# Recurrent layer of a two-layer encoder: two weight remainders ordered behind the first two convolutions, and the first block's gates 2 to 4 steps later

## The chip, the cores and the metric

One Trainium2 chip, one core. The metric is the device time of one execution in microseconds (us); lower is better. All arithmetic is in 32-bit floating point: a weight or an activation is split into a rounded part `hi` and a remainder `lo`, and each product is made of three matmuls (hi·hi, hi·lo, lo·hi).

## The reference, cut to what matters

256 tokens of width 2048 pass through two layers. Layer 0 mixes tokens by attention, layer 1 by a recurrent block; each is followed by a gated feed-forward part. The change lies at the start of the recurrent block:

```python
def recurrent_mixer(h, w_in, conv_w, conv_b, w_a, b_a, w_i, b_i, lam, w_out):
    xy = h @ w_in
    xb, yb = jnp.split(xy, 2, axis=-1)
    yb = jax.nn.gelu(yb, approximate=True)
    xb = depthwise_conv_centred(xb, conv_w, conv_b)
    h_fwd = rg_lru(xb, w_a[0], b_a[0], w_i[0], b_i[0], lam[0], reverse=False)
    h_bwd = rg_lru(xb, w_a[1], b_a[1], w_i[1], b_i[1], lam[1], reverse=True)
    out = (h_fwd + h_bwd).astype(h.dtype) * yb
    return out @ w_out
```

`rg_lru` puts xb through two block-diagonal 256x256 products (the gates), sigmoids them, and scans over the tokens.

## The kernel before, in words

The channels of the recurrent layer go in 8 blocks of 256 (`Block`, L945), two tiles of 128 channels each. While TensorE projects the two x tiles and the two y tiles of one round, the gates, decays and scans of the block before are strewn in between. What the steps of the prediction touch:

- **Weights.** `half()` (L218) takes the next half tile of weights (128x1024) from a fixed list. `load_half` (L126) loads it by SyncE's queue into `raw`, ScalarE casts it to `hi` (L141), VectorE makes the remainder `lo` (L143). Each of raw, hi and lo has 5 buffers, so a load waits for the remainder of five halves earlier. A half holds 8 tiles of 128x128; a tile costs three matmuls (L410, L411, L412: hi·hi, hi·lo of the activation, lo·hi), together one **step** of a counter (`step`, L251).
- **First round.** Before any block there is a round that makes only two x tiles (`project_two`, L426), whose sums lie in two PSUM banks. Then a tiny TensorE product (L542) spreads the row norms, and ScalarE copies it to `nrb` (L544).
- **Convolution.** `conv_branch` (L905): VectorE scales the sum by the norm (`cb`, L910), ScalarE makes the first tap (L912), VectorE the other three (L915: two into the accumulator, one into `xc`), then the cast `xs` (L439) and its remainder (L440). The two convolutions of the first round need the norm and so start only after it; their `xs` feed the gates of block 0.
- **Gates.** `Block.gates` (L956): 12 matmuls (L410 to L412 with `xs` and the gate weights `ghi`, `glo`) into a bank `pm`, of which there are 4. Gates, decays, scans and the finish of a block are functions put on a waiting list, each to be issued by TensorE's program a stated number of steps after the block began: `WHEN_FIRST` for block 0, which begins right behind the product that spreads the norm.
- **Order.** TensorE runs in the order in which the code is written. The order on the other engines is chosen at build time by a scheduler, which may be bound by hand: `not_after(i, ahead)` (L118) notes that the remainder (or, with "act", the cast) of the half taken `ahead` halves later must stand behind instruction i on its engine; `settled` (L121) applies it in `load_half`.

## Time and profile before

| what | us |
|---|---|
| median of 3 runs | 1962.69 |
| lowest and highest of them | 1962.0 and 1963.04 |
| span of the profiled execution | 1962.8 |
| TensorE busy in it | 1955.2 |
| VectorE busy | 1737.4 |
| ScalarE busy | 1357.9 |

The profiled execution's own time is its span, the time from its first to its last instruction. TensorE's matmuls are pipelined: one of 128x256 is listed with 0.28 us but the next one starts 0.12 us after it. So a busy TensorE isn't yet one at full speed, and the starts of successive matmuls tell more than their durations. The granted clock is listed beside the busy times of each stretch (1.00 is full speed).

### The profile page before, as it was taken

The page shows a single profiled execution, that of the slowest core. Times are in us where ns is not written, and L with a number is a line of the kernel's source. Part 1 is how long each engine was busy: PE and PEld are TensorE (multiplying, and loading weights), DVE is VectorE, ACT ScalarE, POOL GpSimd, SP SyncE. Part 2 cuts the span into 40 slices and gives each one's busy share as a digit, 9 for nine tenths or more (in the row PEclk, how much of TensorE's full clock was granted, in tenths as well). Part 3 has the DMA queues.
Part 4 walks back from the last instruction along what each step waited for, and adds up shares of the span by engine and source line. Part 5 has one row for each costly group of instructions (what it writes and reads, how often), then busy time and mean ns, then how long its engine had stood idle before and what let it go on. Part 6 is the DMA issues. An engine that isn't in the chain of part 4 may idle for free.

```text
span 1962.8 us, 27715 instructions
## 1 busy us (share of the span) xinstructions
PE 1955.2 (100%) x9641; PEld 1659.9 (85%) x9641; DVE 1737.4 (89%) x2374; ACT 1357.9 (69%) x2075; POOL 233.7 (12%) x333
## 2 busy tenths in 40 slices
PE   9999999999999999999999999999999999999999
PEld 8888888888888888888899998888888888888887
DVE  6777889999999989999778986999998999989997
ACT  6666767665677556777689986767756776567763
POOL 0011000010011100101034331001101010011010
PEclk9999999999999999999999999999999999999999
DMA  8544667687677876776545556567767777777784
GB/s 333 186 147 138 202 204 240 219 258 246 209 246 242 269 245 214 228 234 232 197 166 184 190 166 209 193 203 243 245 233 239 240 240 255 229 245 236 234 261 163
DMA packets 136364, 434.95 MB, mean 222 GB/s; under 512 B 15264, under 2 KB 16160, under 8 KB 135968
## 3 DMA queue, kind: packets, MB, share of 16 engines
q1 hardware_dynamic: 109296, 360.01, 53.3%
q0 software_dynamic: 26784, 73.15, 14.7%
q8 instruction: 76, 1.25, 0.3%
q14 instruction: 64, 0.52, 0.1%
q10 hardware_dynamic: 144, 0.02, 0.0%
HBM read 431.02 MB, written 2.10 MB: 221 GB/s over the span
## 4 chain that ended last, share of the span: by engine, by line
PE 96%; ACT 2%; DVE 1%; issue 1%; DMA 0%; DVEq 0%; ACTq 0%
PE acc L357 60%; PE pm L357 12%; PE acc L273 10%; PE acc L410 3%; PE acc L411 3%; PE acc L412 3%; PE pm L273 1%; PE pm L411 1%; PE pm L412 1%; PE pm L410 1%; ACT tf L871 1%; DVE lo L143 1%; PE pm L748 1%; PE pm L780 1%; PE pm L766 0%
## 5 line engine op out<-in xcount | busy, mean ns | idle before, releaser
L143 DVE TENSOR_TENSOR lo<-raw,hi 128x1024 fp32r<-128x1024 f32 (+1 forms) x613 | 736.7, 1227 | 87.8 <-ACT hi L141 81.9
L141 ACT CAST hi<-raw 128x1024 fp32r<-128x1024 f32 (+1 forms) x613 | 627.4, 1046 | 255.3 <-PE acc L357 93.0
L357 PE MATMUL acc<-hi,xg 128*128 128x512 f32 x1920 | 612.9, 389 | 0.0
L357 PEld LDWEIGHTS acc<-hi,xg 128*128 128x128 f32 x1920 | 360.4, 188 | 74.7
L357 PE MATMUL acc<-hi,act 128*128 128x512 f32 x1258 | 402.1, 390 | 0.8 <-DVE act L879 0.5
L357 PE MATMUL acc<-lo,xg 128*128 128x512 f32 x960 | 373.5, 389 | 0.0
L357 PEld LDWEIGHTS acc<-hi,act 128*128 128x128 f32 x1258 | 236.0, 188 | 50.6 <-DVE act L879 1.4
L357 PE MATMUL acc<-lo,act 128*128 128x512 f32 x629 | 244.8, 389 | 0.0
L357 PEld LDWEIGHTS acc<-lo,xg 128*128 128x128 f32 x960 | 180.2, 188 | 37.5
L327 ACT CAST wxh<-raw 128x1024 fp32r<-128x1024 f32 x93 | 97.8, 1052 | 110.8 <-DVE raw L325 110.8
L871 ACT COPY tf<-tb 32x256 f32<-32x256 f32 x352 | 142.0, 404 | 5.5 <-DVE tb L865 1.6
L410 PE MATMUL acc<-xg,hi 128*128 128x256 f32 x512 | 145.6, 284 | 0.0
L411 PE MATMUL acc<-xg,hi 128*128 128x256 f32 x512 | 145.4, 284 | 0.0
L412 PE MATMUL acc<-xg,lo 128*128 128x256 f32 x512 | 145.2, 284 | 0.0
L357 PEld LDWEIGHTS acc<-lo,act 128*128 128x128 f32 x629 | 118.2, 188 | 23.8
L323 ACT CAST wxh<-wx 128x512 fp32r<-128x512 f32 x93 | 57.7, 621 | 110.4 <-DVE wx L320 78.2
L322 ACT CAST hi<-sr 128x1024 fp32r<-128x1024 f32 x93 | 97.7, 1051 | 39.2 <-PE acc L357 28.4
L329 DVE TENSOR_TENSOR wxl<-raw,wxh 128x1024 fp32r<-128x1024 f32 x93 | 112.7, 1211 | 6.9 <-ACT wxh L327 6.9
L326 DVE TENSOR_TENSOR lo<-sr,hi 128x1024 fp32r<-128x1024 f32 x93 | 113.1, 1216 | 0.0
L305 POOL DMA_DIRECT2D sr<-in_w_up_dram x64 | 35.6, 557 | 651.0 <-DVE lo L326 482.6
L273 PE MATMUL acc<-hi,xg 128*128 128x512 f32 x320 | 109.0, 401 | 0.3 <-ACT hi L141 0.3
L410 PEld LDWEIGHTS acc<-xg,hi 128*128 128x128 f32 x512 | 98.7, 193 | 0.0
(212 smaller groups left out, 3330.4 us busy)
## 6 DMA issues: line engine op xcount, KB each, us to landing
raw<-in_w_gate_dram SPq DMA_DIRECT2D x176, 512.0 KB, 5.4
raw<-in_w_down_dram SPq DMA_DIRECT2D x147, 512.0 KB, 5.5
raw<-in_w_up_dram SPq DMA_DIRECT2D x112, 512.0 KB, 5.6
sr<-in_w_up_dram POOLq DMA_DIRECT2D x64, 512.0 KB, 4.9
raw<-in_w_in_dram SPq DMA_DIRECT2D x64, 512.0 KB, 4.3
raw<-in_w_qkv_dram SPq DMA_DIRECT2D x46, 512.0 KB, 4.4
raw<-in_w_o_dram SPq DMA_DIRECT2D x32, 512.0 KB, 3.5
wx<-in_w_up_dram SPq DMA_DIRECT2D x64, 256.0 KB, 4.7
```

The lines of the kernel that those rows point to most:

```text
L141: newest["cast"] = in_line("act", act.copy(hi[:, sl, :], raw[:, sl, :]))
L143: rest = in_line("dve", dve.tensor_tensor(lo[:, sl, :], raw[:, sl, :], hi[:, sl, :].bitcast(F32), ALU.subtract))
L273: pe.matmul(accs[a], x, wt[:, k, :], start=(k0 + k == 0 and n == 0), stop=(end and k == 1 and n == 2))
L322: in_line("act", act.copy(hi, raw))
L326: settled(in_line("dve", dve.tensor_tensor(lo, raw, hi[:].bitcast(F32), ALU.subtract)), taken[0] - 1)
L327: in_line("act", act.copy(xh[:, 1:, :], r1))
L329: in_line("dve", dve.tensor_tensor(xl[:, 1:, :], r1, xh[:, 1:, :].bitcast(F32), ALU.subtract))
L357: pe.matmul(acc, a, b, start=id(acc) not in begun, stop=last and i == 2)
L410: pe.matmul(o, hi, x[:, :S], start=start, stop=False)
L411: pe.matmul(o, hi, x[:, S:], start=False, stop=False)
L412: pe.matmul(o, lo, x[:, :S], start=False, stop=stop)
L871: n = act.copy(f[32 * i : 32 * i + 32, q::4, :, :], b[32 * q : 32 * q + 32, :, i, :, :])
```

## The change

Two edits. In `conv_branch`, for the first two channel tiles (ct 0 and 1), the first tap on ScalarE and the remainder of `xs` on VectorE are now noted by `not_after(..., 3)`: the cast and the remainder of the fourth weight half after that point stand behind them on ScalarE and VectorE. In `WHEN_FIRST`, the first three gates of block 0 are issued after 28, 34 and 38 steps and no longer after 24, 30 and 36; the fourth stays at 42, and so does all that follows it.

```diff
-WHEN_FIRST = (24, 30, 36, 42) + WHEN[4:]
+WHEN_FIRST = (28, 34, 38, 42) + WHEN[4:]
...
     def split(dst, src):
         i = dve.tensor_copy(dst[:, :S], src)
-        dve.tensor_tensor(dst[:, S:], src, dst[:, :S].bitcast(F32), ALU.subtract)
+        newest["split"] = dve.tensor_tensor(dst[:, S:], src, dst[:, :S].bitcast(F32), ALU.subtract)
         return i
...
         xc = tmp("xc", bufs=4)
-        act.activation(run, b[:, 0:S], AF.Identity, bias=col("conv_b", ct), scale=col("conv_w", ct))
+        i = act.activation(run, b[:, 0:S], AF.Identity, bias=col("conv_b", ct), scale=col("conv_w", ct))
+        if ct < 2:
+            not_after(i, 3, "act")
         for k in range(1, 4):
             o = xc if k == 3 else run
             dve.scalar_tensor_tensor(o, b[:, k : k + S], col("conv_w", KT * k + ct), run, ALU.mult, ALU.add)
         xs = tmp("xs", (P, 2 * S), F32R, bufs=4)
-        split(xs, xc)
+        i = split(xs, xc)
+        if ct < 2:
+            not_after(newest["split"], 3)
         return xc, xs
```

The numbers of the tiles in the rows below are running numbers of the program; a few change with the order. The four weight halves that matter here are hi_9019/lo_9020 (now hi_8994/lo_8995), hi_9087/lo_9088 (now hi_9062/lo_9063), hi_9142/lo_9143 and hi_9207/lo_9208.

VectorE, from the remainder of the third half after the first round; xs_8850 and xs_8862 are the two operands of the gates, cb_8841 and cb_8853 the inputs of their convolutions. Before:

```order
L143 TENSOR_TENSOR lo_9020<-raw_9018,hi_9019 128x1024
L910 TENSOR_TENSOR cb_8841<-acc_8714,nrb_8836 128x256
L910 TENSOR_TENSOR cb_8853<-acc_8715,nrb_8836 128x256
L143 TENSOR_TENSOR lo_9088<-raw_9086,hi_9087 128x1024
L915 SCALAR_TENSOR_TENSOR acc_8714<-cb_8841,pk,acc_8714 128x256
L143 TENSOR_TENSOR lo_9143<-raw_9141,hi_9142 128x1024
L915 SCALAR_TENSOR_TENSOR acc_8714<-cb_8841,pk,acc_8714 128x256
L915 SCALAR_TENSOR_TENSOR acc_8715<-cb_8853,pk,acc_8715 128x256
L915 SCALAR_TENSOR_TENSOR xc_8845<-cb_8841,pk,acc_8714 128x256
L143 TENSOR_TENSOR lo_9208<-raw_9206,hi_9207 128x1024
L915 SCALAR_TENSOR_TENSOR acc_8715<-cb_8853,pk,acc_8715 128x256
L439 CAST xs_8850<-xc_8845 128x256
```

One remainder of a weight half stands ahead of the two convolutions and three between their steps. VectorE at the same place now, where the steps follow directly on the two cb (lines behind the change are 2 or 4 higher, so L917 is the former L915):

```order
L917 SCALAR_TENSOR_TENSOR acc_8714<-cb_8841,pk,acc_8714 128x256
L917 SCALAR_TENSOR_TENSOR acc_8715<-cb_8853,pk,acc_8715 128x256
L917 SCALAR_TENSOR_TENSOR acc_8714<-cb_8841,pk,acc_8714 128x256
L917 SCALAR_TENSOR_TENSOR acc_8715<-cb_8853,pk,acc_8715 128x256
L917 SCALAR_TENSOR_TENSOR xc_8845<-cb_8841,pk,acc_8714 128x256
L917 SCALAR_TENSOR_TENSOR xc_8857<-cb_8853,pk,acc_8715 128x256
L439 CAST xs_8850<-xc_8845 128x256
L439 CAST xs_8862<-xc_8857 128x256
L440 TENSOR_TENSOR xs_8850<-xc_8845,xs_8850 128x256
L440 TENSOR_TENSOR xs_8862<-xc_8857,xs_8862 128x256
L143 TENSOR_TENSOR lo_8995<-raw_8993,hi_8994 128x1024
L143 TENSOR_TENSOR lo_9063<-raw_9061,hi_9062 128x1024
```

The two convolutions stand in one piece, ahead of them only the two cb; the four remainders that stood ahead of or between their steps (and a fifth, lo_9246, ahead of the last two) now follow them.

TensorE, at the first gate of block 0: acc_8962 is the sum of the second x tile of the round, pm_8993 (now pm_9011) the bank of the first gate. Before:

```order
L411 MATMUL acc_8962<-xg_8472,hi_8964 128x256
L412 MATMUL acc_8962<-xg_8472,lo_8965 128x256
L410 MATMUL pm_8993<-xs_8850,ghi_8866 128x256
L411 MATMUL pm_8993<-xs_8850,ghi_8866 128x256
L412 MATMUL pm_8993<-xs_8850,glo_8865 128x256
```

The first gate follows on the last matmul of the third half. TensorE at the same place now:

```order
L411 MATMUL acc_8962<-xg_8472,hi_8964 128x256
L412 MATMUL acc_8962<-xg_8472,lo_8965 128x256
L410 MATMUL acc_8962<-xg_8591,hi_8994 128x256
L411 MATMUL acc_8962<-xg_8591,hi_8994 128x256
L412 MATMUL acc_8962<-xg_8591,lo_8995 128x256
```

Four tiles of the fourth half (12 matmuls) now stand ahead of the first gate, and the third matmul of them is the first that needs a remainder which now stands behind the convolutions. The number of matmuls is the same.

## The prediction

> **What bounds the kernel now.** I read the head of the page first, then who waited for whom on TensorE, then the granted clock by stretches, and last the instructions of the one place that stood out.

> ```profile
> span 1962.8 us, 27715 instructions
> PE 1955.2 (100%) x9641; PEld 1659.9 (85%) x9641; DVE 1737.4 (89%) x2374; ACT 1357.9 (69%) x2075; POOL 233.7 (12%) x333
> ```

> TensorE (PE) is busy throughout, so only what makes TensorE stop or run slowly can move the end. Its waits in the whole run, by total (engine, line, for whom: us, times, longest):

> ```profile
> PE pm L410 <- DVE xs L439: 0.9, 1, 0.9
> PE pm L411 <- DVE xs L440: 0.7, 1, 0.7
> PE acc L357 <- DVE act L879: 0.5, 2, 0.3
> PE acc L357 <- DVE gl L925: 0.3, 1, 0.3
> ```

> The two longest after the start are one place: the first gate of block 0 waits for the two `xs` that VectorE makes behind the first two convolutions. Stretches around it (us, busy time and count of each engine, granted TensorE clock, DMA share, GB/s):

> ```profile
> 968.00:970.50 2.50, 2.50 (x23) 2.50 (x22) 2.02 (x5) 0.86 (x1) 0.13 (x2) 1.00 0.98 365
> 970.50:974.00 3.50, 1.69 (x7) 0.82 (x6) 3.50 (x10) 1.51 (x2) 0.13 (x2) 0.87 0.79 308
> 974.00:976.00 2.00, 2.00 (x9) 2.00 (x10) 1.52 (x4) 0.13 (x1) 0.25 (x2) 0.50 0.71 242
> 976.00:978.00 2.00, 2.00 (x12) 2.00 (x11) 0.00 (x0) 1.97 (x3) 1.27 (x1) 0.50 0.05 20
> 978.00:979.60 1.60, 1.60 (x9) 1.60 (x9) 0.00 (x0) 1.50 (x4) 0.00 (x0) 0.50 0.33 86
> 979.60:982.00 2.40, 2.40 (x21) 2.40 (x20) 0.00 (x0) 0.92 (x3) 0.02 (x1) 0.94 0.18 59
> ```

> The clock falls to 0.50 while TensorE waits and stays there after the wait is over. Half-rate time: (1 - 0.87)·2·3.5 = 0.9, then 5.6, then 0.06·2·2.4 = 0.3, in all 6.8 us. TensorE there, matmul by matmul (start, listed duration):

> ```profile
> 970.45 0.28 PE L412 MATMUL acc<-xg,lo 128*128 128x256 f32 x1
> 970.82 0.35 PE L410 MATMUL pm<-xs,ghi 128*128 128x256 f32 x1
> 971.82 0.39 PE L411 MATMUL pm<-xs,ghi 128*128 128x256 f32 x1 [0.65 <-DVE xs L440]
> 972.05 0.28 PE L412 MATMUL pm<-xs,glo 128*128 128x256 f32 x1
> 973.25 0.58 PE L410 MATMUL pm<-xs,ghi 128*128 128x256 f32 x1 [0.93 <-DVE xs L439]
> 973.97 0.58 PE L411 MATMUL pm<-xs,ghi 128*128 128x256 f32 x1
> 974.35 0.41 PE L412 MATMUL pm<-xs,glo 128*128 128x256 f32 x1
> ...
> 979.69 0.37 PE L410 MATMUL pm<-xs,ghi 128*128 128x256 f32 x1
> 979.90 0.28 PE L411 MATMUL pm<-xs,ghi 128*128 128x256 f32 x1
> 980.02 0.28 PE L412 MATMUL pm<-xs,glo 128*128 128x256 f32 x1
> ...
> 981.20 0.28 PE L410 MATMUL acc<-xg,hi 128*128 128x256 f32 x1
> ```

> From 980.02 to 981.20 lie 10 spacings, 0.12 us each: full pace. From 974.35 to 979.69 lie 25 (half a gate, six tiles, the head of the second gate), 0.214 us each: half clock.

> **What the place costs.** Between the starts at 970.45 and 981.20 lie 43 spacings: gate, six tiles (18 matmuls), gate, and one. At 0.12 they take 5.16 us; they took 10.75. The loss is 5.59 us. By parts: waiting, from 970.45 to 974.35 with six spacings, 3.90 - 0.72 = 3.18; half clock, 25 spacings, 5.34 - 3.00 = 2.34; the rest 0.07. So nearly half of it isn't in the list of waits at all.

> **The change part by part.** It removes and adds no matmul. The later gates put 12 matmuls (four tiles, 1.44 us) of the fourth half ahead of the first gate. The bound order lets VectorE do the two convolutions without remainders between. Is `xs` then in time? VectorE and ScalarE before:

> ```profile
> 960.38 3.49 DVE L143 TENSOR_TENSOR lo<-raw,hi 128x1024 fp32r<-128x1024 f32 x3
> 963.79 0.74 DVE L910 TENSOR_TENSOR cb<-acc,nrb 128x256 f32<-128x256 f32 x2
> 964.46 1.21 DVE L143 TENSOR_TENSOR lo<-raw,hi 128x1024 fp32r<-128x1024 f32 x1
> ...
> 967.16 0.87 DVE L915 SCALAR_TENSOR_TENSOR acc<-cb,pk,acc 128x256 f32<-128x256 f32 x2
> ...
> 970.43 0.28 DVE L439 CAST xs<-xc 128x256 fp32r<-128x256 f32 x1
> ...
> 971.77 1.23 DVE L143 TENSOR_TENSOR lo<-raw,hi 128x1024 fp32r<-128x1024 f32 x1
> ...
> 973.50 0.41 DVE L440 TENSOR_TENSOR xs<-xc,xs 128x256 fp32r<-128x256 f32 x1
> ```

> ```profile
> 961.77 0.37 ACT L544 COPY nrb<-pm 128x256 f32<-128x256 f32 x1
> ...
> 964.30 0.57 ACT L912 ACTIVATE acc<-cb,pk 128x256 f32<-128x256 f32 x1 [1.21 <-DVE cb L910]
> ...
> 982.18 1.04 ACT L141 CAST hi<-raw 128x1024 fp32r<-128x1024 f32 x1
> ```

> I roll the new order forward with these rows. Three remainders took 963.79 - 960.38 = 3.41, so two end at 962.65; `nrb` is there at 962.14, so the first cb starts at 962.65. The tap on ScalarE started 0.51 behind its cb (963.79 to 964.30): now 963.16; two of 0.57 end at 964.3. Six taps on VectorE at 0.43 (two in 0.87), the second of them not before 964.3, end at about 966.5; two casts (0.28) and two remainders (0.41) end at 967.8. From below, with starts overlapping as the two cb do (0.67 for the pair against 0.74 listed), it is 967.3. From above I take the old chain without its inserts: from the first cb to the last L440 it took 973.91 - 963.79 = 10.1, in which lay four remainders of 1.2 us; without them 5.3, so 962.65 + 5.3 = 968.0.

> TensorE reaches the first gate at 970.45 + 0.12 + 1.44 = 972.0. So `xs` is ready 4 us early: the 3.18 us of waiting go, and with no gap the clock has no cause to fall, so the 2.34 go too. The edits depend on each other. With the binding alone, `xs` would be there at 968.0 for a gate at 970.57. With the later gates alone, it would be there at 973.91, and 1.9 us of waiting would remain.

> What is late next? The fourth remainder now stands behind the convolutions: 967.8 + 1.2 = 969.0. The third matmul behind 970.45 + 0.12 needs it, at 970.8: 1.8 us of cover (its cast on ScalarE, behind the two taps, ends at 964.3 + 1.04 = 965.3). The fifth remainder ends at 970.2 and is wanted behind four tiles, a gate and four tiles, at 974.9. If the cover were gone, each us late would be a us of TensorE, and the half clock might come back with 2.3.

> Behind these remainders queue the loads into their raw buffers, on SyncE, which runs in order. The first of them feeds the first half of the next block. It was cast at 982.18 (the last row above) and is wanted at 981.20 + 34 steps of 0.36 + two gates of 1.44 = 996.3 before, 990.7 now. Its buffer comes free 969.0 - 963.8 = 5 us later than before; even if the cast moved by all of that, to 987.3, it would be in time. I cost this, SyncE's slightly changed order of gate loads and GpSimd's at nothing; their cover is that 3 us.

> The last thing moved is the work behind the gates. The first bank of block 0 comes free with a scan, and the third gate of block 1 is the first TensorE instruction to need it:

> ```profile
> 1001.45 0.69 DVE L992 TENSOR_TENSOR_SCAN h<-sg,pm 128x256 f32<-128x256 f32 x1
> ...
> 1010.56 0.28 PE L410 MATMUL pm<-xs,ghi 128*128 128x256 f32 x1
> ```

> The scan ends at 1002.14, 8.4 us ahead. The gate now comes at 1010.56 - 5.6 = 1005.0. Even if ScalarE and VectorE gained nothing, 2.8 us would be left. From there on TensorE runs the same instructions 5.6 us earlier, and the waits it had later (0.5 and 0.3 us) are a feature of their own places.

> **The sum.** 3.18 + 2.34 + 0.07 = 5.6 us off the span: 1962.8 - 5.6 = 1957.2. The median lies 0.1 under the span, so **1957.1 us**. Its own range is 1956.4 to 1958.2: downward 0.7 for the other small waits and the spread of the runs (1962.0 to 1963.04); upward a first gate that starts 0.25 late, as the one at 970.82 did for whatever reason, and the same spread.

> [...] The stretches show 6.8 us at 0.50 behind gaps of which the longest listed is 0.93 us. [...]

> **The rivals.** Three more stretches bear on them: the stretch in which block 0's scans run, and most of the time ahead of the place and behind it.

> ```profile
> 990.00:1000.00 10.00, 10.00 (x86) 10.00 (x85) 6.51 (x12) 9.37 (x17) 2.16 (x3) 1.00 0.48 169
> 60.00:960.00 900.00, 899.67 (x4146) 749.17 (x4145) 809.08 (x1112) 609.96 (x966) 86.33 (x130) 1.00 0.68 219
> ...
> 1010.00:1900.00 890.00, 889.42 (x4619) 765.99 (x4618) 799.48 (x1079) 643.48 (x951) 131.18 (x173) 1.00 0.69 223
> ```

> *Only the waiting goes (10%).* The half clock has another cause, or the unprofiled runs hadn't got it. Then the gain is 3.2 us: 1962.7 - 3.2 = 1959.5. For it: the fall is seen in one execution only, and the gaps are short. [...] Against: the fall begins inside the wait, the median of the runs is within 0.1 us of the span that holds it, and nowhere else, over 1790 us, does the clock fall.

> *The wait changes its name (5%).* The remainder lo_8995 comes late and TensorE stops on it instead. With the convolutions taking 1.8 + 3.2 = 5 us longer than I rolled, the wait is as long as the old one, the clock falls as before, and the time is 1962.7. Against: such a chain would need 10 us with nothing in between, which is what it took with four remainders.

> *Slower: the banks of block 0 (5%).* The first three gates come 4, 4 and 2 steps later, the fourth doesn't, so ScalarE gets their sigmoids closer together, the scans are late, and the third gate of block 1 waits for its bank. It decides when the scan ends after 1005.0; a wait of d costs d + 2.3 with the half clock, more than the 5.6 gained when d is above 3.3, that is, when the scan ends after 1008.3, 6.2 us later than before although its first input comes earlier. With d = 8 the time is 1957.1 + 8.0 + 2.3 = 1967.4. For it: ScalarE is busy 9.37 of 10 us there, so it has little room to catch up.

> That the change doesn't do what it says is no rival: the order shows both moves.

> **How the numbers follow.** Forecast 80%, the rivals 10, 5 and 5%. 0.2% is 3.9 us, about what a measurement of this kernel can tell from no change: faster means under 1958.8, slower over 1966.6. Faster: the forecast, 0.80. Same: the first two rivals and most of the third's smaller sizes, 0.16. Slower: 0.04. The range goes from 1956.4 up to 1959.7, which takes in the case of waiting alone and leaves out the other 10%.

> **What would show it.** Right: no TensorE wait for `xs` L439 or L440; clock 1.00 in every stretch from 960 to 1010; the starts of all matmuls there 0.12 apart; the last L440 of the two convolutions ended near 967.8 and the fourth remainder near 969; the span shorter by 5.6. Wrong: a TensorE wait for `lo`, a stretch with the clock under 1, or a wait for a bank at about 1005.

## The result and the profile after

| | median, us | lowest to highest | executions |
|---|---|---|---|
| before | 1961.58 | 1960.27 to 1963.54 | 12 |
| after | 1957.49 | 1956.06 to 1958.36 | 12 |

The ratio is 0.9978, with a 95% interval of 0.9971 to 0.9986: 4.1 us less, 2.7 to 5.7. The forecast was 1957.1 in a range of 1956.4 to 1959.7; as a gain it was 5.6. The absolute number came out closer than the gain, and the two parts of that are taken apart below. One execution in what follows, a twelfth of the kernel with its first gate at step 4, ran at a mean clock of 0.556 and took 3285 us; the numbers leave it out.

The head of the page of after, and who waited for whom on TensorE (engine, line, for whom: us, times, longest):

```profile
span 1955.6 us, 27713 instructions
...
PE 1948.8 (100%) x9641; PEld 1655.7 (85%) x9641; DVE 1737.8 (89%) x2374; ACT 1357.2 (69%) x2075; POOL 233.8 (12%) x333
```

```profile
PE pm L459 <- POOL ones L456: 1.0, 1, 1.0
PE acc L273 <- DVE lo L143: 1.0, 2, 0.8
PE acc L357 <- DVE gl L929: 0.7, 1, 0.7
PE acc L357 <- DVE act L879: 0.6, 2, 0.3
```

Both waits for `xs` are gone, and none of the four that are left lies between 960 and 1010 us. The stretches around the place (us, busy time and count of each engine, granted TensorE clock, DMA share, GB/s):

```profile
968.00:970.50 2.50, 2.50 (x23) 2.50 (x22) 2.50 (x4) 1.52 (x2) 0.00 (x0) 1.00 0.83 282
970.50:974.00 3.50, 3.50 (x32) 3.50 (x31) 2.14 (x4) 2.40 (x4) 1.30 (x1) 1.00 0.94 226
...
960.00:1010.00 50.00, 50.00 (x421) 50.00 (x421) 40.20 (x71) 41.81 (x70) 17.30 (x25) 1.00 0.62 202
```

The clock is 1.00 in all of them. Where the stretch from 970.5 to 974 held 7 matmuls it now holds 32. VectorE of after (start, listed duration, instruction):

```profile
958.40 2.35 DVE L143 TENSOR_TENSOR lo<-raw,hi 128x1024 fp32r<-128x1024 f32 x2
960.68 0.75 DVE L910 TENSOR_TENSOR cb<-acc,nrb 128x256 f32<-128x256 f32 x2
961.79 1.76 DVE L917 SCALAR_TENSOR_TENSOR acc<-cb,pk,acc 128x256 f32<-128x256 f32 x4 [0.37 <-ACT acc L912]
963.46 0.87 DVE L917 SCALAR_TENSOR_TENSOR xc<-cb,pk,acc 128x256 f32<-128x256 f32 x2
964.25 0.49 DVE L439 CAST xs<-xc 128x256 fp32r<-128x256 f32 x2
964.65 0.76 DVE L440 TENSOR_TENSOR xs<-xc,xs 128x256 fp32r<-128x256 f32 x2
965.32 2.36 DVE L143 TENSOR_TENSOR lo<-raw,hi 128x1024 fp32r<-128x1024 f32 x2
```

The convolutions run in one piece and end at 965.41. TensorE of after; the first rows are from its start, 959.15 is the small product behind which block 0 begins, 968.83 the first matmul that needs the fourth remainder, 970.02 the first gate, 1182.68 the one that waits for `gl`, 1951.59 the last:

```profile
6.89 0.40 PE L273 MATMUL acc<-lo,xg 128*128 128x512 f32 x1
7.12 0.62 PE L273 MATMUL acc<-hi,xg 128*128 128x512 f32 x2
...
959.15 0.61 PE L542 MATMUL pm<-ndg,ones 128*128 128x128 f32 x4
...
968.83 0.28 PE L412 MATMUL acc<-xg,lo 128*128 128x256 f32 x1
...
969.91 0.28 PE L412 MATMUL acc<-xg,lo 128*128 128x256 f32 x1
970.02 0.28 PE L410 MATMUL pm<-xs,ghi 128*128 128x256 f32 x1
...
1181.64 0.39 PE L357 MATMUL acc<-hi,act 128*128 128x512 f32 x1
1182.68 0.50 PE L357 MATMUL acc<-hi,act 128*128 128x512 f32 x1 [0.65 <-DVE gl L929]
...
1951.59 0.39 PE L357 MATMUL acc<-hi,act 128*128 128x512 f32 x1
```

The same instructions of before:

```profile
9.36 0.63 PE L273 MATMUL acc<-lo,xg 128*128 128x512 f32 x1
9.79 0.95 PE L273 MATMUL acc<-hi,xg 128*128 128x512 f32 x2
...
961.13 0.61 PE L542 MATMUL pm<-ndg,ones 128*128 128x128 f32 x4
...
1189.26 0.39 PE L357 MATMUL acc<-hi,act 128*128 128x512 f32 x1
1189.98 0.50 PE L357 MATMUL acc<-hi,act 128*128 128x512 f32 x1 [0.33 <-DVE gl L925]
...
1958.83 0.39 PE L357 MATMUL acc<-hi,act 128*128 128x512 f32 x1
```

The reader is to see two things. First, the gate of after starts 0.11 behind the last tile, at full pace. Second, the two traces differ already at their start: matmuls of 128x512 follow each other in 0.43 us in before (9.36 to 9.79) where they do in 0.23 in after (6.89 to 7.12), and before reaches the small product 961.13 - 959.15 = 1.98 us later. That isn't the change's doing: in a second profile of the kernel before (part 1 below) the small product came at 958.79. So the change has to be read from that product to the last matmul: 1958.83 - 961.13 = 997.70 in before, 1951.59 - 959.15 = 992.44 in after, 5.26 us less. The span fell by 7.2.

### The profile page after: what moved, and what is told of

It is laid out like the page before. It is cut to its first block, busy times and chain, and to the rows that moved or that the text cites. A ratio compares the mean times of both kernels' runs of the same rounds, so it can differ in the third digit from the quotient of the medians.

```text
span 1955.6 us, 27713 instructions
## 1 busy us (share of the span) xinstructions
PE 1948.8 (100%) x9641; PEld 1655.7 (85%) x9641; DVE 1737.8 (89%) x2374; ACT 1357.2 (69%) x2075; POOL 233.8 (12%) x333
## 4 chain that ended last, share of the span: by engine, by line
PE 97%; ACT 2%; DVE 1%; issue 0%; DMA 0%; SPq 0%; DVEq 0%; ACTq 0%
PE acc L357 61%; PE pm L357 12%; PE acc L273 10%; PE acc L410 3%; PE acc L411 3%; PE acc L412 3%; PE pm L273 1%; PE pm L412 1%; PE pm L411 1%; PE pm L410 1%; ACT tf L871 1%; PE pm L748 1%; PE pm L780 1%; PE pm L766 0%; DVE lo L143 0%
## 5 line engine op out<-in xcount | busy, mean ns | idle before, releaser
L143 DVE TENSOR_TENSOR lo<-raw,hi 128x1024 fp32r<-128x1024 f32 (+1 forms) x613 | 737.3, 1230 | 91.0 <-ACT hi L141 83.7
L141 ACT CAST hi<-raw 128x1024 fp32r<-128x1024 f32 (+1 forms) x613 | 626.9, 1046 | 248.2 <-PE acc L357 97.0
L357 PE MATMUL acc<-hi,xg 128*128 128x512 f32 x1920 | 612.8, 389 | 0.0
L357 PEld LDWEIGHTS acc<-hi,xg 128*128 128x128 f32 x1920 | 360.4, 188 | 74.6
L357 PE MATMUL acc<-hi,act 128*128 128x512 f32 x1258 | 402.1, 390 | 1.2 <-DVE gl L929 0.7
L357 PE MATMUL acc<-lo,xg 128*128 128x512 f32 x960 | 373.4, 389 | 0.0
L357 PEld LDWEIGHTS acc<-hi,act 128*128 128x128 f32 x1258 | 236.0, 188 | 50.9 <-DVE act L879 1.4
L357 PE MATMUL acc<-lo,act 128*128 128x512 f32 x629 | 244.8, 389 | 0.0
L357 PEld LDWEIGHTS acc<-lo,xg 128*128 128x128 f32 x960 | 180.2, 188 | 37.5
L410 PE MATMUL acc<-xg,hi 128*128 128x256 f32 x512 | 144.8, 283 | 0.0
L411 PE MATMUL acc<-xg,hi 128*128 128x256 f32 x512 | 144.6, 282 | 0.0
L412 PE MATMUL acc<-xg,lo 128*128 128x256 f32 x512 | 144.4, 282 | 0.0
L357 PEld LDWEIGHTS acc<-lo,act 128*128 128x128 f32 x629 | 118.1, 188 | 23.9
L328 DVE TENSOR_TENSOR wxl<-wx,wxh 128x512 fp32r<-128x512 f32 x93 | 63.9, 688 | 39.2 <-ACT wxh L323 39.2
```

The source lines that it names most:

```text
L141: newest["cast"] = in_line("act", act.copy(hi[:, sl, :], raw[:, sl, :]))
L143: rest = in_line("dve", dve.tensor_tensor(lo[:, sl, :], raw[:, sl, :], hi[:, sl, :].bitcast(F32), ALU.subtract))
L357: pe.matmul(acc, a, b, start=id(acc) not in begun, stop=last and i == 2)
L410: pe.matmul(o, hi, x[:, :S], start=start, stop=False)
L411: pe.matmul(o, hi, x[:, S:], start=False, stop=False)
L412: pe.matmul(o, lo, x[:, :S], start=False, stop=stop)
```

## The experiments

After the result my theory was: the gain is the wait for `xs` and the half clock that this wait brings on, both removed by the binding; the rivals were that the half clock has another cause or that it is rare. In the earlier gates of part 4 the profile puts the gate's wait for `xs` down to "issue"; in the run with step 8 the cast of the first `xs` ended at 965.05 and the gate started at 965.15. Three series of runs on three chips, each with its own runs of before.

**1. The kernel before once more.** No edit; it asks how typical the one profile was.

> The unchanged kernel again, timed against itself: ratio 1.000. What it is for: the profiled execution of before had a span of 1962.8 us, the changed kernel's timed runs have times about 1.8 us above their spans, so that execution must have been about 3 us slower than the median of before. Theory A (the half clock behind the wait is in every execution, and only the start differs from run to run): every run lists a mean clock of 0.998, and the new profile shows 0.50 for about 6.8 us behind 970 and a loss of 5.6 us there. Theory B (the half clock comes in some executions, or for one window of 3.4 us in some): some runs list 0.999 or 1.000, and the loss at the place differs between profiles, 3.2 us without it.

Measured: 1962.01 against 1961.59 for the runs of before beside it, ratio 1.0001 (0.9992 to 1.0009). Its profile has the two waits for `xs` again (0.9 and 1.0 us), and these stretches:

```profile
968.20:971.60 3.40, 1.43 (x6) 0.67 (x4) 3.40 (x9) 1.52 (x2) 0.13 (x2) 1.00 0.80 308
971.60:974.00 2.40, 2.36 (x14) 2.36 (x15) 1.59 (x4) 1.07 (x2) 0.65 (x3) 0.67 0.72 229
974.00:976.00 2.00, 2.00 (x12) 2.00 (x12) 0.00 (x0) 1.92 (x4) 0.88 (x1) 0.54 0.04 9
```

Time at half clock: 0.33·2·2.4 + 0.46·2·2.0 = 3.42 us, where the profile that I had predicted from showed 6.8. Each execution lists its mean clock over the span: 0.998 in the profile with 6.8 us, 0.999 in this one, 1.000 in after. One stretch of 3.4 us at half clock takes 0.0009 from a mean over 1960 us. All runs of before that stood beside the three series, sorted by that number:

| mean clock | executions | median time in each series, us |
|---|---|---|
| 1.000 | 29 | 1960.11, 1960.08, 1960.21 |
| 0.999 | 57 | 1961.75, 1961.97, 1961.97 |
| 0.998 | 6 | 1962.97, none, 1963.22 |

Two windows at half clock (stretches of 3.4 us), the case that I priced, are 6 of 92 executions; most have one, and 29 have none. One costs 1.6 to 1.9 us, the second 1.2. The eleven executions of this run itself come on top: three at 1.000, seven at 0.999, one at 0.998; one of the three took 1962.9 us, so the clock isn't all that makes an execution long. That each 0.999 is a window at this place is seen in the profiles only; for the other executions it is inferred.

**2. The binding alone.**

```diff
-WHEN_FIRST = (28, 34, 38, 42) + WHEN[4:]
+WHEN_FIRST = (24, 30, 36, 42) + WHEN[4:]
```

> The bound order alone, gates at 24, 30, 36 as before. My theory: xs is ready about 967.5 in the clock of the old profile, the first gate comes at 970.6, so there is no wait and the gain is the whole of the change's: about 4.1 us under before by the medians, ratio 0.998, clock 1.000, no TensorE wait for xs or lo. Rival (the later gates are needed too): a wait for xs of 1 us or more stays, and the gain is half or less.

Measured: 1957.47, ratio 0.9976 (0.9966 to 0.9987), mean clock 1.000 in all 8 executions. TensorE at the first gate:

```profile
968.74 0.28 PE L412 MATMUL acc<-xg,lo 128*128 128x256 f32 x1
968.86 0.28 PE L410 MATMUL pm<-xs,ghi 128*128 128x256 f32 x1
```

No wait. The binding gives the whole gain (1957.47 where after had 1957.49), and the later gates add nothing that shows.

**3. The later gates alone.** Before, with `WHEN_FIRST = (28, 34, 38, 42)`.

> The later gates alone, weight remainders between the steps of the convolutions as before. My theory: xs is ready at 973.9 in the old profile, the gate comes at 972.0, so about 1.9 us of waiting for L439 and L440 stay; whether the clock falls tells how long a gap it takes: with it about 1.9 + 2.3 us lost, 1.4 us under before; without it 1.9 lost and about 3.7 under the old profile's place. Rival: the gates alone are enough, no wait, the whole gain.

Measured: 1959.15, ratio 0.9985 (0.9976 to 0.9994), mean clock 1.000 in all 11 executions. TensorE:

```profile
970.21 0.28 PE L412 MATMUL pm<-xs,glo 128*128 128x256 f32 x1
971.22 0.38 PE L410 MATMUL pm<-xs,ghi 128*128 128x256 f32 x1 [0.73 <-DVE xs L439]
971.94 0.39 PE L411 MATMUL pm<-xs,ghi 128*128 128x256 f32 x1 [0.34 <-DVE xs L440]
972.17 0.28 PE L412 MATMUL pm<-xs,glo 128*128 128x256 f32 x1
```

From 970.21 to 972.17 lie three spacings: 1.96 - 0.36 = 1.6 us of waiting are left (the prediction: 1.9). They don't bring the clock down. So the later gates by themselves remove half of the waiting and, with it, the half clock.

**4. The stop at the gate by itself, in six sizes.** The changed kernel with its first gate earlier, so that TensorE is there before `xs` is. The other three gates stay.

```diff
-WHEN_FIRST = (28, 34, 38, 42) + WHEN[4:]
+WHEN_FIRST = (8, 34, 38, 42) + WHEN[4:]
```

The first, with step 8:

> The changed kernel with the first gate of block 0 after 8 steps and no longer 28, so that TensorE meets a gap before xs is ready: about 1.8 us for the first xs and 0.4 us for its remainder, 2.2 us in all. Theory A (part of a window of 3.4 us without matmuls makes the clock fall): 0.50 for 3.4 to 6.8 us behind it, loss against the changed kernel 2.2 + 1.2 to 2.4 = 3.4 to 4.6 us, about as slow as before. [...]

Measured: 1961.09, ratio 0.9995 (0.9986 to 1.0004); 9 of 11 executions at 0.999 (median 1961.21), two at 1.000 (1959.28). TensorE, and the stretches:

```profile
963.21 0.28 PE L412 MATMUL acc<-xg,lo 128*128 128x256 f32 x1
965.15 0.35 PE L410 MATMUL pm<-xs,ghi 128*128 128x256 f32 x1 [1.66 <-issue]
965.64 0.58 PE L411 MATMUL pm<-xs,ghi 128*128 128x256 f32 x1
966.02 0.41 PE L412 MATMUL pm<-xs,glo 128*128 128x256 f32 x1
```

```profile
964.00:966.00 2.00, 0.72 (x2) 0.55 (x3) 2.00 (x8) 1.62 (x2) 0.46 (x4) 0.90 0.70 270
966.00:968.00 2.00, 2.00 (x11) 2.00 (x11) 2.00 (x2) 0.00 (x0) 0.00 (x0) 0.50 0.00 0
968.00:970.00 2.00, 2.00 (x15) 2.00 (x15) 1.32 (x2) 1.81 (x2) 1.13 (x1) 0.74 0.75 233
```

A stop of 1.94 - 0.12 = 1.82 us brings 0.40 + 2.00 + 1.04 = 3.44 us at half clock by these rounded rows, and nearly the whole gain is lost.

Step 12:

> The changed kernel with its first gate at step 12 instead of 28. In the run with step 8 the last tile's matmul started at 963.21 and the gate at 965.15, when xs was there: 1.82 us without a matmul. Four steps more are 1.44 us, so 0.4 us are left, and then the small stop of 0.37 us between the gate's first two matmuls. Theory A (a stop of part of a window makes the clock fall, and what counts is how much of the window is idle): some 0.8 us of waiting is less than the 1.6 us that let the clock stand in the run with later gates alone, so 1.00 in the profile and nearly all runs, and 0.8 us above the changed kernel: 1958.3. Theory B (any stop at a gate's head brings a window at half clock): 0.50 for 3.4 us, another 1.2 us, 1959.5.

Measured: 1957.89, ratio 0.9985 (0.9976 to 0.9993), mean clock 1.000 in all 11.

Step 10:

> The changed kernel with its first gate at step 10: one stop of 1.82 - 0.72 = 1.1 us ahead of the gate and 0.37 us in it, 1.5 us in all. Theory A: half clock in few runs or none, since 1.6 us in pieces brought none and 2.2 us brought it in 9 of 11 runs; 1.5 us above the changed kernel, 1959.0. If the length of the longest single stop decides (1.1 us here, 0.9 us in the kernel before with its half clock in 29 of 41 runs): half clock in most runs, 1960.2.

Measured: 1959.0, ratio 0.9989 (0.9980 to 0.9998), mean clock 1.000 in all 11. The stop of 1.09 us was as long as the longest in before (1.08) and brought no half clock, so the longest single stop isn't what decides; step 9 below, with 1.45 us, says it more clearly.

Step 4:

> The changed kernel with its first gate at step 4. [...] Theory A (part of a window is enough, and the more of it is idle, the surer): half clock in every run, one or two windows. The waiting is 3.7 us, of which 0.4 comes back at the later wait for gl, as it did with steps 8 and 10; one window gives 1.3 more, two 2.6: 1962.1 or 1963.4. [...]

Measured: 1962.44, ratio 1.0006 (0.9997 to 1.0015); of 11 executions 8 at 0.999, 3 at 0.998, none at 1.000. The stop ahead of the gate is 3.26 us (the starts at 961.31 and 964.69, less 0.12), with the 0.47 behind it 3.7. The stretches of its profile:

```profile
964.00:966.00 2.00, 1.20 (x5) 1.01 (x6) 2.00 (x6) 0.22 (x1) 0.46 (x4) 0.72 0.52 209
966.00:968.00 2.00, 2.00 (x11) 2.00 (x11) 1.73 (x2) 0.28 (x1) 0.00 (x0) 0.50 0.12 39
968.00:970.00 2.00, 2.00 (x18) 2.00 (x18) 0.00 (x0) 1.97 (x3) 1.29 (x1) 0.92 0.88 305
```

Step 9:

> The changed kernel with its first gate at step 9, between step 10 (1.56 us idle in all, half clock in 0 of 11 runs) and step 8 (2.3 us, 9 of 11): one stop of 1.46 us and 0.47 us more, 1.9 us in all. [...] Waiting alone 1.9 - 0.4 = 1.5 us over the changed kernel, 1959.0; runs with a window 1960.3.

Measured: 1959.26, ratio 0.9990 (0.9982 to 0.9999), mean clock 1.000 in all 11, where I had expected between 1 and 8 of them at half clock. The expectation missed: any 3.4 us here hold at most the 1.9 us that this gate is idle in all, and none of the 11 fell.

The changed kernel as it is, beside these two:

> The changed kernel once more, without an edit, as the base for the two others on this chip: 1957.5, clock 1.00 in all runs, and 4.1 us under the kernel before.

Measured: 1957.15, ratio 0.9979 (0.9970 to 0.9987), mean clock 1.000 in all 11.

Together (idle: time without a matmul at the gate, worked out from the starts; where half clock covers the two small stops inside the gate, those of step 12 are taken, 0.37 and 0.10 us):

| kernel | idle there, us | longest stop | executions below 1.000 |
|---|---|---|---|
| step 12 | 0.84 | 0.37 | 0 of 11 |
| step 10 | 1.56 | 1.09 | 0 of 11 |
| later gates alone | 1.6 | 0.89 | 0 of 11 |
| step 9 | 1.9 | 1.45 | 0 of 11 |
| step 8 | 2.3 | 1.82 | 9 of 11 |
| before | 3.2, spread over 3.8 | 1.08 | 63 of 92 |
| step 4 | 3.7 | 3.26 | 11 of 11 |

The packed traces also list each change of the granted clock, in us from the start of the span. In the four profiles that show a fall:

| profile | first 1.00 | fall to 0.50 | 1.00 again | lengths at 1.00, 0.50, 1.00, in units of 3.4133 us |
|---|---|---|---|---|
| before | 10.50 | 973.06 | 979.88 | 282, 2, 288 |
| before again (part 1) | 6.47 | 972.44 | 975.85 | 283, 1, 288 |
| step 8 | 6.47 | 965.61 | 969.03 | 281, 1, 290 |
| step 4 | 5.74 | 964.89 | 968.30 | 281, 1, 291 |

The third length runs to a fall behind the last matmul. Every length is a whole number of units, so in these four executions the clock changed only at the lines of a grid of 3.4133 us that started at its first rise. In the nine other profiles it doesn't fall ahead of the last matmul. Two pairs of stretches cut at grid lines, the window with the gate and what follows it; the first pair is before, the second step 9:

```profile
969.65:973.06 3.41, 1.93 (x12) 1.35 (x11) 3.41 (x8) 1.51 (x2) 0.13 (x2) 1.00 0.97 380
973.06:979.88 6.82, 6.49 (x28) 6.20 (x29) 2.46 (x7) 3.80 (x6) 1.52 (x3) 0.50 0.37 121
...
961.89:965.30 3.41, 1.99 (x15) 1.62 (x14) 3.41 (x11) 3.16 (x4) 0.46 (x4) 1.00 0.69 246
965.30:968.70 3.40, 3.40 (x30) 3.40 (x30) 3.40 (x4) 2.13 (x3) 1.46 (x1) 1.00 0.31 102
```

From the starts, as in the table above (the listed busy time runs on to each matmul's end), the time without matmuls in the window that ends at the fall is 2.1 us (before), 2.4 (before again), 2.2 (step 8) and 3.3 (step 4). The emptiest window of this length on the grid with no fall behind it is step 9's, with 1.9. So in these profiles the windows that lacked matmuls for 2.1 us or more of their 3.41 were followed by one at half clock, and the one that lacked them for 1.9 wasn't; nothing between the two was tried. In before the first of the two windows at half clock itself lacked matmuls for 0.9 us, in the other three profiles for 0.5 or less, which may be why a second one followed: it is one case.

This may also be what sets the executions of before apart, most of which have no profile: its idle time is spread over 3.8 us, and its place on the grid differs. It began 0.9 us behind a line in before (at 970.57, the line at 969.65) and 2.6 in before again (968.23 and 965.61), and in before the line at 973.06 cut it in two, 2.1 and 0.9. An estimate from the starts of before again: if every place of the grid were equally likely, its gaps would bring half clock in 56 to 69% of executions, for limits from 2.14 down to 1.93 us; 63 of 92 are 68%. The same estimate for step 8 is 38 to 50%, and 9 of 11 fell, so which places are likely stays open.

**5. The cover of the fourth remainder.** One more VectorE instruction, a sum that nobody uses, between the last `xs` and the fourth remainder of the weights: 1024 elements a partition (below) and 3072.

```diff
+        if ct == 1:
+            pad = tmp("pad", (P, 2), bufs=1)
+            tok = x_tok[:].rearrange("p a c f -> p (a c f)")[:, :1024].rearrange("p (a f) -> p a f", a=2)
+            not_after(follow(dve.tensor_reduce(pad, tok, AX.X, ALU.add), newest["split"]), 3)
```

> The changed kernel with one more VectorE instruction, a sum over 1024 elements that nobody uses, bound between the last remainder of xs and the fourth remainder of the weights. It takes about 1.1 us and so makes the fourth remainder end 1.1 us later, at about 967.6, where the tile that reads it is wanted at 968.83. Theory A (the cover of the fourth remainder is 2.3 us): no wait for lo, no loss, 1957.5 and a verdict of no difference. Theory B (the chain of the convolutions is as tight as it was before, rival two of the prediction): a wait of about 1 us for lo, 1958.5 or more.

Measured: 1957.64, ratio 0.9986 (0.9977 to 0.9995), mean clock 1.000. The sum delayed the fourth remainder by 1.13 us, to an end at 968.13, and TensorE ran through. With 3072 elements:

> The same with a sum over 3072 elements that nobody uses, about 3.3 us, 1.0 us more than the cover. Theory A: TensorE stops for about 1.0 us for lo at the matmul that reads the fourth remainder, the time is 1958.5, and the clock stands at 1.00, since 1.0 us is less idle time than the 1.6 us that left it. The prediction's price (each us late is a us of TensorE, and with the half clock 2.3 more) would give 1960.8.

Measured: 1959.2, ratio 0.9990 (0.9982 to 0.9999), mean clock 1.000 in all 11. VectorE:

```profile
965.67 3.34 DVE L925 TENSOR_REDUCE pad<-x_tok 128x2 f32<-128x3072 f32 x1
968.94 1.22 DVE L143 TENSOR_TENSOR lo<-raw,hi 128x1024 fp32r<-128x1024 f32 x1
```

TensorE, at the tile that reads the fourth remainder, and 215 us later:

```profile
969.05 0.28 PE L411 MATMUL acc<-xg,hi 128*128 128x256 f32 x1
970.20 0.39 PE L412 MATMUL acc<-xg,lo 128*128 128x256 f32 x1 [0.87 <-DVE lo L143]
...
1183.33 0.39 PE L357 MATMUL acc<-hi,act 128*128 128x512 f32 x1
1185.46 0.51 PE L357 MATMUL acc<-hi,act 128*128 128x512 f32 x1 [1.74 <-DVE gl L933]
```

The stop for `lo` is 1.15 - 0.12 = 1.03 us, as worked out from a cover of 2.3 (the remainder of after ended near 966.5 and was wanted at 968.83), and it brings no half clock. But 1959.2 is above the 1958.5 that I expected: the matmul that waits for `gl` comes 2.13 us behind the one ahead of it, where the spacing was 1.04 in the profile of after. Held against the second profile of the changed kernel instruction by instruction, from the small product on, VectorE and ScalarE are 2.5 to 4.4 us late (medians of 10 us each) from 20 us behind that product on and 2.9 late at `gl`; TensorE, only 1 us late until then, ran into it. It isn't a backlog of VectorE alone, which stands idle for 2.8 us waiting for ScalarE shortly ahead of that `gl`: the two run late together.

## Why the prediction was right, point by point

**The place: right.** From the small product to the matmul ahead of the later wait for `gl` it took 228.1 us in before (961.13 to 1189.26) and 222.5 in after (959.15 to 1181.64). The difference, 5.64, is the 5.59 of the prediction.

**The roll forward: right within half a us.** In the clock of before, 1.98 later, `xs` was ready at 967.4 (forecast 967.8, from 967.3 to 968.0), the gate started at 972.0 (972.0), and the fourth remainder was ready at about 968.5 (969.0). Its cover was put at 1.8 us. The padded kernel gives 2.24: its fourth remainder started 3.27 us behind the sum (965.67 to 968.94) and TensorE stopped for 1.03.

**The waiting: right in size.** 3.18 us. Runs of before without half clock lie 1960.21 - 1957.15 = 3.1 above after in the last series, 2.6 in the first (1960.11 - 1957.47, by the binding alone).

**The half clock: the mechanism right, the size not.** 2.34 us was what the one profiled execution had lost. It had two windows, which 6 of 92 executions have. Averaged over the table of executions, with the medians of its rows some 1.8 and 3.0 us above the first, the half clock is (57·1.8 + 6·3.0) / 92 = 1.3 us. So the gain is 3.1 + 1.3 = 4.4, not 5.6; the series with both kernels gave 4.1 and 1961.70 - 1957.15 = 4.55.

**The conversion to the median: wrong, and it cancelled.** "The median lies 0.1 under the span" joined the span of one execution to the times of three others. Each execution's time is about 1.8 us above its own span (after: 1957.33 over 1955.6), so the profiled execution of before took about 1964.6, an estimate: its own time isn't on record. Against that stood its slow start, which cost 2 us and was not the change's doing. The forecast span of 1957.2 came out as 1955.6, 1.6 lower, the time 1.8 above it: two errors of one size. That the absolute time came out within 0.4 us is luck.

**The later waits: not quite "a feature of their own places".** The spacing at the wait for `gl` was 0.72 in before and 1.04 in the profile of after, but 0.62 in the second profile of after. It differs by 0.42 between two executions of one kernel, more than between the two kernels' first profiles, so nothing is charged to it.

**The later gates: a needless part.** I wrote that the edits depend on each other. They don't: the binding alone has `xs` ready in time, and by the prediction's own numbers (968.0 for a gate at 970.57) it had to.

**The rivals.** The case of waiting only fell with the half clock in 63 of 92 executions and the step 8 kernel. One argument against it was weaker than I read it: two stretches of some 900 us printed as 1.00 don't show that the clock fell nowhere else, since one window takes only 0.002 from such a mean. The trace's list does show it: between 10.50 us and the last matmul of before it has the one fall at 973.06. The late remainder fell with 2.2 us of cover; its price was too high, since a stop of 1.03 us brought no half clock in 11 executions, and too low, since the lateness of VectorE came back at `gl` (2.13 us from matmul to matmul for 1.04). The banks of block 0 were no matter: the scan that frees the first one ended at 995.81 (it started at 995.12 and took 0.69) and the third gate of block 1 started at 1002.94, 7.1 us later, against 8.4 before.

## What to carry to other kernels

At a gap on TensorE, add up the time without matmuls, in pieces too, over 3.41 us, the unit of all lengths at one clock in these traces. In this kernel up to 1.9 us cost only itself; with 2.1 us or more within one window of the grid another 1.6 to 1.9 came behind it, and 1.2 more where a second window followed. Before pricing what one profile shows, look how often the other executions show it, here by their mean clock, and compare two traces from a common instruction and not from their starts. A step that was made earlier by reordering one engine leaves that engine's other work late: its cover is known only when it has been padded until it breaks.
